# Strassen pairs for the mixer's in and out projections in a hybrid decoder layer

## Chip, cores and metric

One NeuronCore of a Trainium2 chip runs the whole kernel. The metric is the device time of one execution in microseconds (us). The engines are named as in the profile: PE is TensorE (PEld its weight loads), DVE is VectorE, ACT is ScalarE, POOL is GpSimd and SP is SyncE, which issues most DMAs.

## What is computed

One layer of a hybrid decoder on 256 tokens, with model width 2048 and FFN width 5632:

```python
x = x + 0.5 * swiglu(rmsnorm(x, ffn1_norm), w_gate1, w_up1, w_down1)   # FFN 1
h = rmsnorm(x, mix_norm)
a_q, a_k, a_v, m_q, m_k, m_v, m_o, m_i, m_f = split(h @ w_in)          # in projection
y_a = diff_attention(a_q, a_k, a_v, lam)    # 4 heads, causal, two softmaxes a head, RMSNorm
y_b = mlstm(silu(conv(m_q, m_k)), m_v, gates(m_i, m_f)) * sigmoid(m_o) # 4 heads, conv over 4 tokens
x = x + concat(y_a, y_b) @ w_out                                       # out projection
x = x + 0.5 * swiglu(rmsnorm(x, ffn2_norm), w_gate2, w_up2, w_down2)   # FFN 2
out = rmsnorm(x, final_norm)
```

All arrays are float32. The part between the two FFNs is called the mixer here.

## The kernel before

**Products.** The 256 tokens are two blocks of 128. An activation is kept transposed, as sixteen K tiles of 128 features (44 for the FFN's inner width). A product takes a 128x128 piece of the activation as the stationary operand and 512 columns of a weight, and adds into a PSUM bank of 512 columns (tag `acc`, six banks). Every operand is split in two, a rounded high part and the remainder, and each product is three matmuls: high by high, high by low, low by high (`mm3`, lines 141 to 143). Two tiles of K are a unit (UK = 2). For each unit of 512 columns, SP loads 128x1024 values of weight, ACT casts them to the high part `wh` (L113), and DVE subtracts to get the low part `wl` (L114). A transposed activation gets its parts from L108/L109 (with a gain) or L113/L114.

**Strassen pairs.** The FFNs use `Paired` (L322). It takes two weight chunks `wa` and `wb` of 512 columns and, over the first 2·ns of the K tiles, multiplies the 2x2 blocks (two token blocks by two adjacent K tiles, and two K tiles by two weight chunks) with seven block products where eight are needed plainly. The rest of K is plain. For this DVE forms sums of weight tiles, `sums` (L350) and a second sum in place (L352), which are then split like weights; a POOL DMA that adds while it copies (L361) makes a third one. The activations are needed as eight combinations, `xs`, formed by `sum_pair` (ACT `xg`/`hg`, three `xsum` operations at L273 to L275, then casts and subtractions into `xs`) in place of the two plain tiles `xt`. `combine` (L364) has six operations on the four banks of products.

**The chain.** `Chain.run` (L444) works off one pair: the first four products of each of the ns K pairs (`first`, on banks p5, p7, p1, p6), with the previous pair's `third` (the plain rest of its `wb`) between them; then `combine`; then `second` (the remaining three products, and the plain rest of `wa`), whose result goes to a function `half`; and the pair's own `third` goes into the chain for the next run. `pending` is a list of transposes that `flush` runs at one later point, so that TensorE doesn't wait for what they transpose.

**The mixer.** None of its projections is a pair. `linear` and `units` (L174, L213) work off one chunk of 512 columns after the other, each sixteen K tiles by two token blocks, 96 instructions of 128x512: three narrower chunks `wqk` (m_q, m_k and the gates), ten chunks `win`, four chunks `wout`. The mLSTM and the attention stand between the chunks: the convolution on DVE (L626 to L629), the gates between units of the first two `win` chunks, the scores (L774 to L788) and numerators (L799 to L810) of all four heads after them, the attention's scores and softmax (L833 to L867) after the q and k chunks, its weighting (L885 to L899) after the v chunks, and the gated output (L903 to L917). `rsq` (L224) raises to the power -1/2 on POOL.

**Order.** Each engine runs its instructions in program order, and a tile scheduler sets this order from the order of the code and from priorities: what stands under `tc.high_priority(offset=AHEAD)` (loads, splits) is moved ahead by up to 400 places. Pools set how far ahead work can go: 4 tiles `raw` of 1 MB, 5 `rawp` of 512 KB (which `sums` also takes), 4 split weight tiles in `wsp`, 2 banks `ps_tr` for transposes, 6 `ps_acc`.

## Time and profile before

| | us |
|---|---|
| median of three runs | 1829.08 |
| the three runs | 1822.75, 1829.08, 1830.97 |
| the profiled execution | 1824.08 |
| its span, first to last instruction | 1822.4 |
| mean granted TensorE clock in it | 0.998 |

The span is what the trace covers; 1.7 us of the profiled execution lie around it. In the trace FFN 1 runs until about 700 us, the in projection and the attention until about 1025, the out projection until about 1130, and FFN 2 from there on. Line numbers of rows are those of the kernel before. The profile's duration of an instruction reaches from its start to its end, and the next one on the engine often starts before that end; where the pace of an engine is wanted, starts are compared.

### The profile page before, as it was taken

Reading aid. Unit: us, or ns where it says so; the run is one execution under the profiler, and the core shown is the slowest. Engines: PE = TensorE matmul, PEld = TensorE weight load, DVE = VectorE, ACT = ScalarE, POOL = GpSimd, SP = SyncE. Lnnn points to the kernel's source line nnn. Section 1 sums busy time; section 2 is a strip of 40 time slices with the busy share of each in tenths; the row PEclk is TensorE's granted clock in tenths of the full one; section 3 lists DMA queues with packets and bytes.
Section 4 is the critical chain, followed back from the end, with each engine's and each line's share of the span. In section 5 each row is a group of like instructions: output and inputs, shape, how many; then the busy total and the mean of one; then the engine's idle time right before and its main releaser. Section 6 shows DMA issues by size and latency. Waiting matters only on the chain.

```text
span 1822.4 us, 22684 instructions
## 1 busy us (share of the span) xinstructions
PE 1794.6 (98%) x8090; PEld 1468.2 (81%) x8090; DVE 1488.8 (82%) x1775; ACT 1121.7 (62%) x1443; POOL 156.3 (9%) x199
## 2 busy tenths in 40 slices
PE   8999999999999999999999999999999999999998
PEld 6788788878887888978888888788787888887886
DVE  6889889988998887674465578899889988998886
ACT  6666666666666666554455456666666666666664
POOL 0001100111002100000000000101110021002100
PEclk9999999999999999999999999999999999999999
DMA  8667877797688874553544565677877798678864
GB/s 333 215 204 235 222 234 232 246 250 220 210 252 247 259 237 146 200 185 121 185 159 164 185 213 179 199 228 241 234 230 225 256 247 243 208 230 256 253 190 155
DMA packets 114449, 397.72 MB, mean 218 GB/s; under 512 B 12960, under 2 KB 12960, under 8 KB 107424
## 3 DMA queue, kind: packets, MB, share of 16 engines
q1 hardware_dynamic: 88560, 349.28, 55.5%
q0 software_dynamic: 24480, 44.58, 14.2%
q10 hardware_dynamic: 1296, 2.42, 0.4%
q8 instruction: 63, 1.03, 0.2%
q14 instruction: 50, 0.41, 0.1%
HBM read 349.56 MB, written 2.10 MB: 193 GB/s over the span
## 4 chain that ended last, share of the span: by engine, by line
PE 76%; DMA 9%; DVE 8%; issue 4%; ACT 2%; SPq 1%; POOL 0%; POOLq 0%; DVEq 0%; ACTq 0%
PE acc L142 24%; PE acc L143 24%; PE acc L141 24%; DMA raw<-in_wu_dram 6%; DVE wl L114 5%; ACT wh L113 2%; DVE sums L350 2%; DMA raw<-raw 1%; PE tr L296 1%; SPq L166 1%; DMA xres<-in_x_dram 1%; DVE raw L352 1%; DMA xraw<-in_xt_dram 1%; DMA raw<-in_wd_dram 0%; PE num L808 0%
## 5 line engine op out<-in xcount | busy, mean ns | idle before, releaser
L113 ACT CAST wh<-raw 128x1024 fp32r<-128x1024 f32 (+3 forms) x503 | 464.3, 931 | 377.2 <-PE acc L143 360.9
L114 DVE TENSOR_TENSOR wl<-raw,wh 128x1024 fp32r<-128x1024 f32 (+3 forms) x503 | 535.1, 1074 | 194.7 <-ACT wh L113 191.1
L142 PE MATMUL acc<-wl,xt 128*128 128x512 f32 (+3 forms) x1632 | 630.4, 386 | 4.2 <-DVE wl L114 4.0
L141 PE MATMUL acc<-wh,xt 128*128 128x512 f32 (+3 forms) x1632 | 630.7, 387 | 2.6 <-ACT xt L108 1.5
L143 PE MATMUL acc<-wh,xt 128*128 128x512 f32 (+3 forms) x1632 | 628.8, 386 | 1.2 <-DVE xt L109 1.2
L114 DVE TENSOR_TENSOR wl<-rawp,wh 128x1024 fp32r<-128x1024 f32 x284 | 346.7, 1222 | 43.8 <-ACT wh L113 37.1
L113 ACT CAST wh<-rawp 128x1024 fp32r<-128x1024 f32 x284 | 298.8, 1053 | 117.1 <-PE acc L143 96.4
L141 PE MATMUL acc<-wh,xs 128*128 128x512 f32 x902 | 355.7, 397 | 8.4 <-ACT wh L113 4.0
L142 PEld LDWEIGHTS acc<-wl,xt 128*128 128x128 f32 x1632 | 306.5, 188 | 67.9 <-DVE wl L114 8.8
L141 PEld LDWEIGHTS acc<-wh,xt 128*128 128x128 f32 x1632 | 306.0, 188 | 65.5 <-ACT wh L113 2.8
L143 PEld LDWEIGHTS acc<-wh,xt 128*128 128x128 f32 x1632 | 306.3, 188 | 62.1 <-DVE xt L109 2.5
L142 PE MATMUL acc<-wl,xs 128*128 128x512 f32 x902 | 352.7, 391 | 1.3 <-DVE wl L114 1.1
L143 PE MATMUL acc<-wh,xs 128*128 128x512 f32 x902 | 350.9, 390 | 0.1
L113 ACT CAST wh<-sums 128x1024 fp32r<-128x1024 f32 x122 | 128.4, 1053 | 144.4 <-PE acc L143 139.2
L141 PEld LDWEIGHTS acc<-wh,xs 128*128 128x128 f32 x902 | 169.1, 188 | 57.2 <-ACT u L371 9.3
L142 PEld LDWEIGHTS acc<-wl,xs 128*128 128x128 f32 x902 | 169.4, 188 | 38.9 <-DVE wl L114 6.4
L143 PEld LDWEIGHTS acc<-wh,xs 128*128 128x128 f32 x902 | 169.3, 188 | 36.0 <-DVE xs L109 1.0
L361 POOL DMA_DIRECT2D raw<-raw x122 | 104.0, 853 | 1030.9 <-DVE wl L114 973.7
L350 DVE TENSOR_TENSOR sums<-raw 128x1024 f32<-128x1024 f32 x122 | 149.2, 1223 | 39.4 <-DMA raw<-in_wu_dram 29.2
L114 DVE TENSOR_TENSOR wl<-sums,wh 128x1024 fp32r<-128x1024 f32 x122 | 149.0, 1222 | 14.7 <-ACT wh L113 14.7
L352 DVE TENSOR_TENSOR raw<-sums,raw 128x512 f32<-128x512 f32 x122 | 83.8, 687 | 0.5
L282 POOL DMA_DIRECT2D xres<-part x48 | 43.6, 1060 | 238.2 <-ACT part L281 238.2
(194 smaller groups left out, 756.0 us busy)
## 6 DMA issues: line engine op xcount, KB each, us to landing
rawp<-in_wd_dram SPq DMA_DIRECT2D x96, 512.0 KB, 5.7
rawp<-in_wu_dram SPq DMA_DIRECT2D x94, 512.0 KB, 7.6
raw<-in_wg_dram SPq DMA_DIRECT2D x89, 512.0 KB, 6.7
rawp<-in_wg_dram SPq DMA_DIRECT2D x86, 512.0 KB, 5.7
raw<-in_wu_dram SPq DMA_DIRECT2D x82, 512.0 KB, 7.5
raw<-in_wd_dram SPq DMA_DIRECT2D x80, 512.0 KB, 6.3
raw<-in_win_dram SPq DMA_DIRECT2D x40, 1024.0 KB, 4.8
raw<-raw POOLq DMA_DIRECT2D x122, 256.0 KB, 6.3
```

The lines of the kernel that those rows point to most:

```text
L113: nc.scalar.copy(hi, src)
L114: nc.vector.tensor_tensor(out=lo, in0=src, in1=hi.bitcast(F32), op=ALU.subtract)
L141: nc.tensor.matmul(acc, lh, rh, start=first, stop=False, skip_group_check=on)
L142: nc.tensor.matmul(acc, lh, rl, start=False, stop=False, skip_group_check=on)
L143: nc.tensor.matmul(acc, ll, rh, start=False, stop=last, skip_group_check=on)
L166: nc.sync.dma_start(dst, w[k // LK][:, k % LK:k % LK + 2, :])
L282: nc.gpsimd.dma_start(xres[:, hb, c * CW:(c + 1) * CW], t, accum_op=ALU.add)
L296: nc.tensor.transpose(tr[:, i, hb * P:(hb + 1) * P], hs[hb][:, k * P:(k + 1) * P], ident)
L350: nc.vector.tensor_tensor(out=sums, in0=raw[:, 0:4:3, :], in1=raw[:, 2:3, :].to_broadcast([P, 2, CW]), op=ALU.add)
L352: nc.vector.tensor_tensor(out=raw[:, 2, :], in0=sums[:, 0, :], in1=raw[:, 3, :], op=ALU.add)
L361: nc.gpsimd.dma_start(raw[:, 2, :], raw[:, 1, :], accum_op=ALU.add)
```

## The change

The in and out projections become Strassen pairs in the chain, as in the FFNs, with four K pairs each (NP_MIX = NP_OUT = 4: K tiles 0 to 7 by seven products, 8 to 15 plain). The ten `win` chunks are five pairs, run in the order (2,3) for a_q, (0,1) for m_v, (4,5) for a_k, (6,7) for a_v, (8,9) for the gates m_o; the four `wout` chunks are two. The first two `wqk` chunks stay plain and the third is the stream that the first pair takes between its products. The narrow chunks keep their number of instructions.

The steps of mLSTM and attention become entries of two lists: `side` (convolution of a head, gate steps) is taken up between units of `first` and `second`, and `mid` (scores, numerators, attention and weighting of one head) after each unit of `second`. Their operations on ACT and DVE go through `vec` and `act`, which raise their priority above that of the splits. Transposes in `pending` are run one per unit. The convolution's first tap moves from DVE to ACT, and the gates' small products from `ps_acc` to `ps_tr`.

`finish1` asks `chunk_to_xt` for the combinations `xs` in place of plain `xt` for half of the K tiles of the in projection, and `y_transposes` does it for the attention's four heads. In the `wout` pairs (`by_dma`) the second weight sum isn't made by DVE: ACT copies the first sum into place (L377 after) and a POOL DMA adds the other part onto it (L378 after), and the split of it is issued after the chain's unit.

```diff
+NP_MIX = 4
+NP_OUT = 4
...
-    def flush():
-
-        for f in pending:
+    def flush(n=None):
+
+        now = pending[:n]
+        del pending[:n]
+        for f in now:
             f()
...
-                sum_pair(xp, j, gained(tr, gbase + 2 * j))
+                sum_pair(xp, j, gained(tr, prm[:, gbase + 2 * j:gbase + 2 * j + 2]))
...
-            nc.scalar.activation(g[:, i * S:(i + 1) * S], src[:, i, :], AF.Copy,
-                                 scale=prm[:, gcol + i:gcol + i + 1])
+            act.activation(g[:, i * S:(i + 1) * S], src[:, i, :], AF.Copy, scale=gain[:, i:i + 1])
...
+    class Early:
+
+
+        def __init__(self, engine):
+            self.engine = engine
+
+        def __getattr__(self, op):
+            def run(*args, **kwargs):
+                with soon():
+                    return getattr(self.engine, op)(*args, **kwargs)
+
+            return run
+
+    vec, act = Early(nc.vector), Early(nc.scalar)
+    side, mid = [], []
+
+    def aside(work):
+
+        if work:
+            work.pop(0)()
+
...
                     nc.vector.tensor_tensor(out=sums, in0=raw[:, 0:4:3, :],
                                             in1=raw[:, 2:3, :].to_broadcast([P, 2, CW]), op=ALU.add)
-                    nc.vector.tensor_tensor(out=raw[:, 2, :], in0=sums[:, 0, :], in1=raw[:, 3, :], op=ALU.add)
-                    e = pair_tiles(wsp, "w", [P, 2, CW])
+                    if self.by_dma:
+                        nc.scalar.copy(raw[:, 2, :], sums[:, 0, :])
+                        nc.gpsimd.dma_start(raw[:, 2, :], raw[:, 3, :], accum_op=ALU.add)
+                    else:
+                        nc.vector.tensor_tensor(out=raw[:, 2, :], in0=sums[:, 0, :], in1=raw[:, 3, :], op=ALU.add)
+                        e = pair_tiles(wsp, "w", [P, 2, CW])
                     split(sums, *f)
-                    split(raw[:, 0:3:2, :], *e)
+                    if not self.by_dma:
+                        split(raw[:, 0:3:2, :], *e)
                 self.prod(self.p5, j, S1, f, 0, at, end)
                 self.prod(self.p7, j, S3, f, 1, at, end)
+                if self.by_dma:
+                    yield
+                    with tc.high_priority(offset=AHEAD):
+                        e = pair_tiles(wsp, "w", [P, 2, CW])
+                        split(raw[:, 0:3:2, :], *e)
                 self.prod(self.p1, j, A1, e, 0, at, end)
                 self.prod(self.p6, j, S2, e, 1, at, end)
                 with tc.high_priority(offset=AHEAD):
                     nc.gpsimd.dma_start(raw[:, 2, :], raw[:, 1, :], accum_op=ALU.add)
-                yield
+                if not self.by_dma:
+                    yield
 
         def combine(self):
...
+                aside(side)
                 if i < self.ns:
                     bare(i)
                     if i % 2 or i == self.ns - 1:
                         upper(i - i % 2)
                 if i < len(self.rest):
                     self.plain(self.wa, self.rest[i], (n11, n21))()
-                if i == 0:
+                if i % 2 == 0:
                     flush()
+                aside(mid)
             return [n11, n21]
 
         def third(self, last_units=1):
...
+        def run(self, p, half, end, last_units=1, lead=()):
 
             done = 0
+            for f in lead:
+                next(self.stream)
+                done += 1
+                f()
             for i, _ in enumerate(p.first()):
                 while done < (i + 1) * self.steps // p.ns:
                     next(self.stream)
                     done += 1
+                flush(1)
+                aside(side)
             p.combine()
             self.end()
             half(p.second())
...
-        pending.append(functools.partial(chunk_to_xt, c, G_MIX, xp2, 0))
+        pending.append(functools.partial(chunk_to_xt, c, G_MIX, xp2, NP))
...
+    def conv(acc, src, h, i):
+        w = lambda j: prm[:, G_CW + j * 8 + i:G_CW + j * 8 + i + 1]
+        a = acc[:, h, :]
+        act.activation(a, src[:, h, :], AF.Identity, scale=w(3), bias=prm[:, G_CB + i:G_CB + i + 1])
+        for d in (1, 2, 3):
+            vec.scalar_tensor_tensor(a[:, d:], src[:, h, :S - d], w(3 - d), a[:, d:], op0=ALU.mult, op1=ALU.add)
+        act.activation(a, a, AF.Silu)
...
+    accs = []
+    chain.put(units(accs, xp2, wqk[2], KD, fine=True), KD // UK, functools.partial(finish_qk, 2, accs))
...
-        mb = ps_acc.tile([P, CW], F32, tag="acc", name="mb")
+        mb = ps_tr.tile([P, CW], F32, tag="tr", name="mb")
...
+    def both(c):
+        return Paired(xp2, win[c], win[c + 1], KD, NP_MIX)
+
+    mq, mk = (mixt([P, NH, S], name="cv") for _ in range(2))
+    for i in range(2 * NH):
+        side.append(functools.partial(conv, (mq, mk)[i // NH], mT[i // NH], i % NH, i))
+    for i, f in ((1, gates_sum), (3, gates_scan), (5, gates_max)):
+        side.insert(i, f)
+    qT, kT = [], []
+    chain.run(both(2), to_T(qT), to_T(qT))
+
...
+    by_head(scores)
+    chain.run(both(0), functools.partial(take_mv, 0), functools.partial(take_mv, 1))
+    by_head(numerators)
+    chain.run(both(4), to_T(kT), to_T(kT))
...
+        pending_T.append(functools.partial(weights_T, h, w))
...
+            pending.extend([f for f in pending_T] + [lambda: mid.extend(weigh)])
...
+        if kt // 2 < NP_OUT:
+            sum_pair(yT, kt // 2, gained(tr, g))
+            return
...
+        later.append(functools.partial(y_transposes, [y[:, hb, :] for hb in range(NT)], 2 * h, gatt))
...
+    by_head(attend)
+    chain.run(both(6), take_av, take_av)
+    chain.run(both(8), functools.partial(gate_out, 0), functools.partial(gate_out, 1))
+    pending[:0] = later
...
-    for c in range(4):
-        accs = []
-        chain.put(units(accs, yT, wout[c], KD, fine=c == 3), KD // UK, functools.partial(finish_out, c, accs))
-        if c < 3:
-            chain.finish()
+    for c in (0, 2):
+        chain.run(Paired(yT, wout[c], wout[c + 1], KD, NP_OUT, by_dma=True), functools.partial(finish_out, c),
+                  functools.partial(finish_out, c + 1),
+                  lead=() if c else [functools.partial(flush, 1)] * 2)
```

Three places in the order of instructions, each word for word.

On TensorE where the out projection begins, before: `acc_8264` and `acc_8263` are the last chunk of the in projection, `tr_8318` and `tr_8328` the first transposes of attention outputs (`ya`).

```order
L142 MATMUL acc_8264<-wl_8302,xt_6003 128x512
L143 MATMUL acc_8264<-wh_8301,xt_6003 128x512
L877 MATMUL tr_8318<-ident,ya_8212 128x128 x4
L877 MATMUL tr_8328<-ident,ya_8228 128x128 x4
L141 MATMUL acc_8263<-wh_8357,xt_6013 128x512
L142 MATMUL acc_8263<-wl_8358,xt_6013 128x512
```

The same place after: `acc_8355` is the last bank of the gate pair's `third`, `acc_8859` and `acc_8858` are the first products of the first `wout` pair, on the combinations `xs_8810` and `xs_8811` made of the first head's transposes (`tr_8802`, thirteen rows further up).

```order
L145 MATMUL acc_8355<-wh_8822,xt_6238 128x512
L945 MATMUL tr_8838<-ident,ya_8671 128x128 x4
L945 MATMUL tr_8877<-ident,ya_8715 128x128 x4
L945 MATMUL tr_8923<-ident,ya_8771 128x128 x4
L945 MATMUL tr_8987<-ident,yb_8777 128x128 x4
L143 MATMUL acc_8859<-wh_8863,xs_8810 128x512
L144 MATMUL acc_8859<-wl_8864,xs_8810 128x512
L143 MATMUL acc_8858<-wh_8863,xs_8810 128x512
L144 MATMUL acc_8858<-wl_8864,xs_8810 128x512
L145 MATMUL acc_8859<-wh_8863,xs_8811 128x512
```

Three heads' transposes and the first of the mLSTM's now stand in a row right ahead of the first products that use such combinations; before, plain products of the in projection's last chunk follow two of them.

On DVE at that place, before: splits of the last chunk's weights (`wl`), and plain low parts `xt` of the attention outputs.

```order
L114 TENSOR_TENSOR wl_8410<-raw_8407,wh_8409 128x1024
L882 SCALAR_TENSOR_TENSOR xt_8317<-tr_8318,gatt,xt_8317 128x256
L882 SCALAR_TENSOR_TENSOR xt_8327<-tr_8328,gatt,xt_8327 128x256
L882 SCALAR_TENSOR_TENSOR xt_8317<-tr_8318,gatt,xt_8317 128x256
L882 SCALAR_TENSOR_TENSOR xt_8327<-tr_8328,gatt,xt_8327 128x256
L114 TENSOR_TENSOR wl_8426<-raw_8407,wh_8425 128x1024
L882 SCALAR_TENSOR_TENSOR xt_8337<-tr_8338,gatt,xt_8337 128x256
L882 SCALAR_TENSOR_TENSOR xt_8347<-tr_8348,gatt,xt_8347 128x256
```

After: the splits of the first `wout` pair's weights, and the combinations (`xs`, `xsum`) of four heads.

```order
L116 TENSOR_TENSOR wl_8910<-sums_8911,wh_8909 128x1024
L116 TENSOR_TENSOR xs_8811<-xg_8807,xs_8810 128x512
L116 TENSOR_TENSOR wl_8942<-raw_8906,wh_8941 128x1024
L275 TENSOR_TENSOR xsum_8814<-xg_8807 128x256
L276 TENSOR_TENSOR xsum_8814<-xsum_8814,xg_8807 128x128
L277 TENSOR_TENSOR xsum_8814<-xg_8807,xsum_8814 128x128
L275 TENSOR_TENSOR xsum_8850<-xg_8843 128x256
L276 TENSOR_TENSOR xsum_8850<-xsum_8850,xg_8843 128x128
L116 TENSOR_TENSOR xs_8847<-xg_8843,xs_8846 128x512
L277 TENSOR_TENSOR xsum_8850<-xg_8843,xsum_8850 128x128
L275 TENSOR_TENSOR xsum_8889<-xg_8882 128x256
L116 TENSOR_TENSOR xs_8811<-xsum_8814,xs_8810 128x512
```

Where two low parts were formed for a pair of K tiles, five instructions stand now, between splits that the first products wait for.

On POOL, before, from the mLSTM's norm to FFN 2's first pair: `rmh` and four `ra` alone.

```order
L224 TENSOR_TENSOR rmh_7149<-rsqv_7147,mhalf 128x8
L224 TENSOR_TENSOR ra_8210<-rsqv_8208,mhalf 128x2
L224 TENSOR_TENSOR ra_8226<-rsqv_8224,mhalf 128x2
L224 TENSOR_TENSOR ra_8242<-rsqv_8240,mhalf 128x2
L224 TENSOR_TENSOR ra_8258<-rsqv_8256,mhalf 128x2
L361 DMA raw_9148<-raw_9148 128x512
```

After, the same stretch up to the second `wout` pair: L378 is the added DMA of `by_dma`, L395 the DMA that makes the third sum, L227 the power for a head's norm.

```order
L378 DMA raw_8860<-raw_8860 128x512
L227 TENSOR_TENSOR ra_8613<-rsqv_8611,mhalf 128x2
L378 DMA raw_8906<-raw_8906 128x512
L227 TENSOR_TENSOR ra_8669<-rsqv_8667,mhalf 128x2
L227 TENSOR_TENSOR ra_8713<-rsqv_8711,mhalf 128x2
L378 DMA raw_8952<-raw_8952 128x512
L378 DMA raw_9008<-raw_9008 128x512
L395 DMA raw_8860<-raw_8860 128x512
L227 TENSOR_TENSOR ra_8769<-rsqv_8767,mhalf 128x2
L395 DMA raw_8906<-raw_8906 128x512
L395 DMA raw_8952<-raw_8952 128x512
L395 DMA raw_9008<-raw_9008 128x512
```

Four DMAs of `by_dma` stand ahead of the first L395 of that pair, and `ra` of the attention heads stands between them.

## Rows read from the trace of the kernel before

**Rows 1.** The page: busy time of each engine, its share of the span and its instructions; then the chain of work that ended last, by engine.

```profile
PE 1794.6 (98%) x8090; PEld 1468.2 (81%) x8090; DVE 1488.8 (82%) x1775; ACT 1121.7 (62%) x1443; POOL 156.3 (9%) x199
...
PE 76%; DMA 9%; DVE 8%; issue 4%; ACT 2%; SPq 1%; POOL 0%; POOLq 0%; DVEq 0%; ACTq 0%
```

**Rows 2.** What TensorE waited for over the whole run: line, what it waited for: us in total, times, longest.

```profile
PE acc L142 <- DVE wl L114: 5.1, 12, 0.8
PE acc L141 <- ACT wh L113: 4.9, 9, 0.7
PE acc L141 <- ACT xs L108: 2.0, 2, 1.5
```

**Rows 3.** The same view, from 705 to 1120 us, which is the mixer without its last part: all that it lists.

```profile
PE tr L242 <- DVE xt L109: 0.2, 1, 0.2
```

**Rows 4.** Busy time of each engine in stretches: the first FFN's middle, the mixer up to its last part, the last part of the output projection with the hand-over to the second FFN, the second FFN's middle. Columns: stretch and its length, then PE, PEld, DVE, ACT and POOL busy us (instructions), the granted TensorE clock (1.00 is 2.4 GHz, 0.50 is 1.2 GHz), DMA share, GB/s.

```profile
250.00:700.00 450.00, 447.12 (x1985) 364.90 (x1984) 404.33 (x446) 288.82 (x344) 48.02 (x60) 1.00 0.79 236
705.00:1120.00 415.00, 414.72 (x2003) 349.08 (x2002) 250.50 (x385) 221.62 (x346) 8.90 (x12) 1.00 0.50 172
1120.00:1165.00 45.00, 43.03 (x189) 33.95 (x188) 37.76 (x44) 27.75 (x36) 4.65 (x5) 1.00 0.63 192
1165.00:1700.00 535.00, 531.09 (x2358) 434.07 (x2357) 487.37 (x537) 346.78 (x411) 61.82 (x73) 1.00 0.78 234
```

**Rows 5.** TensorE's timeline in an input-projection chunk: start, duration, line, tile. A matmul's records overlap; the starts of those left out lie between the rows shown at the same pace, and the last row is the 44th after the first.

```profile
803.74 0.39 PE L141 MATMUL acc<-wh,xt 128*128 128x512 f32 x1
803.97 0.40 PE L142 MATMUL acc<-wl,xt 128*128 128x512 f32 x1
804.20 0.39 PE L143 MATMUL acc<-wh,xt 128*128 128x512 f32 x1
...
813.50 0.39 PE L142 MATMUL acc<-wl,xt 128*128 128x512 f32 x1
813.73 0.39 PE L143 MATMUL acc<-wh,xt 128*128 128x512 f32 x1
```

**Rows 6.** The two FFN stretches again, with the instructions on tiles named acc alone (columns as above; the count behind PE is that of the matmuls).

```profile
250.00:700.00 450.00, 442.09 (x1921) 357.69 (x1920) 46.68 (x71) 33.23 (x56) 1.00 0.79 236
1165.00:1700.00 535.00, 525.43 (x2286) 425.95 (x2285) 50.25 (x77) 40.70 (x70) 1.00 0.78 234
```

**Rows 7.** The same for tiles named tr, the 128x128 transposes.

```profile
250.00:700.00 450.00, 8.28 (x64) 7.46 (x64) 5.91 (x9) 8.97 (x16) 1.00 0.79 236
1165.00:1700.00 535.00, 9.31 (x72) 8.41 (x72) 5.91 (x9) 10.11 (x18) 1.00 0.78 234
```

**Rows 8.** Three stretches around the mLSTM's scores and numerators, which stand between two projection chunks (columns as in the stretches above, with the granted clock behind POOL).

```profile
814.00:822.00 8.00, 8.00 (x39) 5.34 (x39) 2.90 (x4) 4.44 (x13) 0.00 (x0) 0.99 0.52 196
822.00:825.20 3.20, 3.20 (x10) 2.55 (x10) 1.05 (x3) 0.61 (x3) 0.00 (x0) 0.50 0.00 0
825.20:829.00 3.80, 3.80 (x20) 3.34 (x18) 2.77 (x12) 0.00 (x0) 0.00 (x0) 1.00 0.00 0
```

**Rows 9.** VectorE's timeline inside a Strassen pair of the second FFN, instructions back to back.

```profile
1183.85 1.22 DVE L114 TENSOR_TENSOR wl<-rawp,wh 128x1024 fp32r<-128x1024 f32 x1
1184.99 1.22 DVE L350 TENSOR_TENSOR sums<-raw 128x1024 f32<-128x1024 f32 x1
1186.12 0.29 DVE L275 TENSOR_TENSOR xsum<-hg,xsum 128x128 f32<-128x128 f32 x1
1186.33 0.69 DVE L352 TENSOR_TENSOR raw<-sums,raw 128x512 f32<-128x512 f32 x1
1186.93 1.22 DVE L114 TENSOR_TENSOR wl<-sums,wh 128x1024 fp32r<-128x1024 f32 x1
1188.06 1.22 DVE L114 TENSOR_TENSOR wl<-raw,wh 128x1024 fp32r<-128x1024 f32 x1
```

**Rows 10.** VectorE's groups of equal instructions: line, operation, out<-in, shapes xcount | busy us, mean ns of one | idle before.

```profile
L372 DVE TENSOR_TENSOR acc<-acc,u 128x512 f32<-128x512 f32 x37 | 25.6, 693 | 0.5 <-ACT u L371 0.5
L114 DVE TENSOR_TENSOR xs<-xsum,xs 128x512 fp32r<-128x512 f32 x28 | 19.0, 686 | 0.0
L109 DVE SCALAR_TENSOR_TENSOR xt<-tr,prm,xt 128x256 fp32r<-128x256 f32 x24 | 10.6, 479 | 0.6 <-ACT xt L108 0.5
L273 DVE TENSOR_TENSOR xsum<-hg 128x256 f32<-128x256 f32 x20 | 8.4, 420 | 0.0
L626 DVE TENSOR_SCALAR cv<-mT,prm 128x256 f32<-128x256 f32 x8 | 3.2, 407 | 0.0
L898 DVE TENSOR_SCALAR ya<-av,ra 128x256 f32<-128x256 f32 x8 | 3.5, 480 | 3.4 <-POOL ra L224 3.4
```

**Rows 11.** The same view of ScalarE.

```profile
L113 ACT CAST wh<-rawp 128x1024 fp32r<-128x1024 f32 x284 | 298.8, 1053 | 117.1 <-PE acc L143 96.4 <-ACT wh L113 10.5 <-issue 2.3
L113 ACT CAST wh<-raw 128x512 fp32r<-128x512 f32 x132 | 77.9, 620 | 87.6 <-PE acc L143 86.1 <-DMA raw<-in_wg_dram 1.5
L371 ACT COPY u<-acc 128x512 f32<-128x512 f32 x37 | 21.4, 579 | 0.6 <-DVE acc L370 0.4
L257 ACT ACTIVATE xg<-tr,prm 128x256 f32<-128x256 f32 x8 | 3.3, 467 | 0.0
```

**Rows 12.** GpSimd's instructions on tiles named raw (the DMAs that add one quarter of a weight tile onto another, all from L361): ns of one min/median/max, first and last start; then the time from issue to landing.

```profile
L361 POOL DMA_DIRECT2D raw<-raw x122: 841/854/1038, 44.4 to 1780.5; - x122
DMA to landing us min/median/max: 3.3/6.3/9.9
```

More of the change, by code (lines that the diff above doesn't have):

```diff
@@ L168, in load_unit @@
     def load_unit(w, k):
-        raw = wrp.tile([P, UK, CW], F32, tag="rawp", name=nm("rawp"))
+        raw = wrp.tile([P, UK, w.shape[3]], F32, tag="rawp", name=nm("rawp"))
         with tc.high_priority(offset=AHEAD):
@@ L538, in sum_xt @@
         raw, j, hi, lo = gs.pop(0)
-        sums(gained(raw, G_FFN1 + j * UK), hi, lo)
+        sums(gained(raw, prm[:, G_FFN1 + j * UK:G_FFN1 + j * UK + UK]), hi, lo)
     parts1 = small.tile([P, NT, 4], F32, tag="parts", name="parts1")
@@ L750, in gates_max, with take_mv, scores @@
             mcol = ct([P, 8], "mcol")
-            nc.vector.tensor_tensor(out=mcol, in0=mm[:, 0:8], in1=bcol[:, 0:8], op=ALU.add)
+            vec.tensor_tensor(out=mcol, in0=mm[:, 0:8], in1=bcol[:, 0:8], op=ALU.add)
             enm = ct([P, 8], "enm")
-            nc.scalar.activation(enm, mcol, AF.Exp, scale=-1.0)
+            act.activation(enm, mcol, AF.Exp, scale=-1.0)
         late.update(enm=enm)
-    mq = conv_silu(mT[0], 0)
-    mk = conv_silu(mT[1], 4)
-    between = {(0, 4): gates_sum, (0, 6): gates_scan, (1, 4): gates_max}
     mv = {}
-    for j in range(2):
-        accs = linear(xp2, win[j], KD, ahead=lambda u: between.get((j, u), lambda: None)())
+    def take_mv(j, accs):
         for hb in range(NT):
-            t = mixt([P, 2, VD + 1], name="mv")
+            t = work.tile([P, 2, VD + 1], F32, tag="w", name=nm("mv"))
             mv[j, hb] = t
             nc.gpsimd.memset(t[:, :, VD:VD + 1], 1.0)
-            nc.scalar.activation(t[:, :, 0:VD], accs[hb].rearrange("p (a b) -> p a b", a=2), AF.Copy,
+            act.activation(t[:, :, 0:VD], accs[hb].rearrange("p (a b) -> p a b", a=2), AF.Copy,
                                  scale=rstd2()[:, hb:hb + 1])
-    gcol, gx, nsel, mrow, enm = (late[n] for n in ("gcol", "gx", "nsel", "mrow", "enm"))
+    def both(c):
[7 more added lines that the diff above has]
+    chain.run(both(2), to_T(qT), to_T(qT))
     sws = []
-    for h in range(NH):
+    def scores(h):
+        gcol, gx, nsel, mrow = (late[n] for n in ("gcol", "gx", "nsel", "mrow"))
         rr = ps_acc.tile([P, CW], F32, tag="acc", name=nm("rr"))
@@ L822, in tile_trunk_layer, with attend @@
     fm = ct([P, 8], "fm")
[L823 to L830 removed]
+    vec.tensor_tensor(out=fm, in0=rmh, in1=dd, op=ALU.mult)
     sca = DK ** -0.5
[L832 to L833 removed]
+    wts, weigh = {}, []
+    def attend(h):
         q, k, o = qT[h // 2], kT[h // 2], 2 * (h % 2)
```

206 lines of the change are left out of this document (95 added, 111 removed).

## Prediction

> **What bounds the kernel now.** First the page's totals and its chain of waits: TensorE is busy for 98% of the span, and 76% of the chain that ended last is PE [rows 1]. VectorE, 82% busy, is next. So the first question is how many matmul slots the change removes, the second whether the other engines still keep ahead. The list of what TensorE waited for has no entry of weight [rows 2], and in the mixer nearly none at all: 0.2 us in 415 [rows 3]. The stretches show why. In the mixer DVE is busy for 250.50 of 415 us (60%) and ACT for 221.62 (53%), while the FFNs, which run on Strassen pairs already, have DVE at 404.33 of 450 and 487.37 of 535 (90 and 91%) [rows 4]. The FFN stretches are thus the best picture of what the mixer becomes.
>
> **What a matmul slot is worth.** Records overlap, so the pace is read from starts: 803.74 to 813.73 is 9.99 us for 44 steps, 0.227 us each [rows 5]. A pair of chunks needs 16 K tiles x 2 chunks x 2 token blocks x 3 = 192 instructions plainly. As a pair with four K pairs it needs 4 x 7 x 3 = 84, and 8 x 2 x 2 x 3 = 96 for the plain rest, 180 together. Seven pairs save 84 instructions: 84 x 0.227 = **-19.1 us**. All of this lies on the path, since PE is what never waits there.
> The row's pace is that of a stream in which every matmul has a weight load of its own. The Trainium skill ("TensorE: Matmul & The Clock Gate", section "Back-to-back issue gap") gives about 131 ns as the sustained spacing of matmuls with 512 columns, and about 216 ns as an isolated one. By 131 ns the 84 would bring 11.0 us and the sum below would be 8.1 us higher; the trace speaks against it, and for the page's other figure, with 44 equal steps of 227 ns.
>
> **The clock.** Between two chunks the scores and numerators of all heads stand in a row, and in 822.0 to 825.2 the granted clock is 0.50, which is 1.2 GHz, after a stretch at 0.99 that was filled with narrow matmuls; behind it the clock is 1.00 again [rows 8]. After the change each head's scores and numerators follow a unit of full-width products. I expect the drop not to come: half of 3.2 us, **-1.6 us** (bounds 0 and -1.6).
>
> **Stalls where DVE is tight.** In the first FFN stretch 450 us hold 1921 wide matmuls, 1921 x 0.227 = 436.1, and 8.28 us of transposes; 5.6 us are left over. In the second: 535 - 2286 x 0.227 - 9.31 = 6.8 [rows 6, 7]. Both are 1.25% of the stretch. The mixer pays nearly nothing of that now. Is its DVE load going to be like theirs? Back to back, a DVE instruction starts 0.08 us before the last one's end: 1.14 us for 128x1024, 0.60 for 512 columns, 0.21 for the small `xsum` [rows 9]. A pair in the in projection has per K pair `sums`, the second sum, two splits of 1024, later one more split of 1024 and one of 512: 4 x 1.14 + 2 x 0.60 = 5.76, four times 23.0; eight plain units 9.1; `combine` 4 x 0.61 = 2.4 [rows 9, 10]. That is 34.6 us beside 180 x 0.227 = 40.9 of PE, where the two plain chunks had 16 x 1.14 = 18.2: +16.3 a pair. A `wout` pair leaves out the second sum, 4 x 0.60, and has +13.9. Five and two pairs: +109. Eight activation pairs change from two `xt` (0.40 each) to two `xs` and three `xsum` (2 x 0.60 + 0.34 + 2 x 0.21 = 1.96): +9.3. The convolution's first tap leaves DVE, 8 x 0.33 = -2.6 [rows 10]. So about +116 on 250.5, 366 us in a stretch that shrinks to some 404: 91%, the FFNs' load. ACT gains the casts and copies for the same tiles (1.05, 0.62, 0.58 and 0.47 us [rows 11]), about +77 on 221.6, 74%: not the bound on average. I therefore give the mixer the FFNs' share: 1.25% of 400 = **+5 us** (bounds 0 and 12: none, as now, or 16 steps of the heads that each cost one of the longest single waits seen, 0.8 us [rows 2]).
>
> **The start of the out projection.** Here the work isn't like the FFNs'. The first `wout` pair needs sums of attention outputs that come from transposes just ahead, and the order has four groups of transposes in a row, through two banks, then the first products. I count from the order, from the first TensorE row that uses the unit before the last of the gate pair's rest up to the end of the first part of that `wout` pair: 96 wide matmuls and 24 transposes (8.28 / 64 = 0.13 us each [rows 7]), 21.8 + 3.1 = 24.9 us. DVE has in that time 12 splits and 2 `sums` of 1024 (16.0), eight `xs` parts (4.8), four groups of `xsum` (3.0), ten operations of 256 columns (4.0) and two tiny ones (0.2): 28.0 us. DVE is 3.1 us behind if it starts level. Before, TensorE had plain products there, and what waited was DVE, for `ra` on POOL, 3.4 us in four waits [rows 10]. POOL now issues four adding DMAs (0.85 us each [rows 12]) among these `ra`, and each delay of one passes on to `ya`, the transposes and the sums. I take **+3 us** (bounds 0, if DVE enters with tiles ready, and 8: the 3.1, the four `ra` waits of 3.4 and one or two POOL issues of 0.85 in front).
>
> **The two ends.** At FFN 1's end the transposes of the first two chunks of x feed four `sum_pair`s and not plain tiles, inside the last pair of FFN 1: 4 x 1.16 = 4.6 us more on a DVE that is 90% busy, most of it ahead of need: **+1** (0 to 3). At the hand-over to FFN 2 the stretch of 45 us has 43.03 of PE [rows 4], so 2 us are lost already; the last `wout` chunk's rest still ends inside FFN 2's first pair, now beside sums and a `combine` on DVE: **+1** (-2, if nothing is lost there any more, to 3). Loads cost nothing: the weight bytes are the same, and the DMA share in the mixer is 0.50 where the FFNs run at 0.79 with loads of the same size [rows 4]. The 36 further POOL DMAs at 0.85 us are 31 us on an engine with 9% load [rows 1, 12].
>
> **Sum against the profiled execution:** -19.1 - 1.6 + 5 + 3 + 1 + 1 = -10.7, so 1824.08 becomes 1813.4. The three runs before lie on average 3.5 us above it (1827.6; their median 5.0 above). I add 3.5: **1817 us**, case A.
>
> **Rivals.**
> B, the stalls don't come: the steps of the heads fill what DVE leaves, and DVE enters the out projection with work in hand. For it: the three longest entries of TensorE's waits sum to 12 us in the whole run [rows 2], fewer than 1.25% of it. Against: every stretch on pairs shows its 1.25%. -19.1 - 1.6 = -20.7: 1803.4, with 3.5 about 1807.
> C, bursts: sixteen steps (scores, numerators, attention, weighting of four heads) stand on TensorE in line between wide products, and each has an answer from ACT or DVE that the next one needs. Their raised priority puts them ahead of splits, and a split that is late stops TensorE. Now such steps wait in the plain mixer for little [rows 3], since DVE has 40% free; at 91% it hasn't. At 0.5 us a step, between 0.2 [rows 3] and 0.8 [rows 2], this is 8 us more: 1821.4, with 3.5 about 1825, no difference that counts.
> D, slower, by `by_dma`: the second sum of a `wout` unit takes an ACT copy (0.58), a POOL issue (0.85), the landing (6.3 in the median, 3.3 to 9.9), a cast (1.05) and a split (1.22), 10.0 us in a row [rows 9 to 12], while TensorE has 24 x 0.227 = 5.45 us of work per unit. If POOL's queue or the five `rawp` tiles keep these from running ahead, each unit costs 4.5 us and eight cost 36: 1850, about 1853. It decides from five such units on (5 x 4.5 = 22 above A's 1817 is 0.5% over the old time). Against: the order puts four of these DMAs ahead of the first other one in the first `wout` pair, so they run ahead of the products that need them.
> The Trainium skill ("SBUF — State Buffer", section "SBUF: two separate sides") warns that a DMA issued from GpSimd can starve while VectorE holds the port that they share, and that would lengthen D's chain with VectorE at 91%. In the FFNs, at 90%, the trace has the issue at 841 to 1038 ns throughout, which leaves D's terms as they are.
> That the change doesn't do what it says is ruled out by the instructions: 84 fewer wide matmuls stand in its order.
>
> **Chances.** A 0.45, B 0.17, C 0.28, D 0.10. About 0.5% (9.1 us) is what a measurement of this kernel can tell from no change: below 1820 is faster, above 1838 slower. A lies near that bound, and 0.08 of its 0.45 falls inside; C all but does. Faster 0.37 + 0.17 = 0.54, same 0.08 + 0.28 = 0.36, slower 0.10. The range goes from B less the 4 us that runs scatter, 1803, to C with the start of the out projection at its upper bound, 1825 + 5 + 2 = 1832.
>
> **What would show it.** In the stretches after: the mixer's PE near its length, DVE near 90% there, and no 0.50 clock at the scores. TensorE's waits in the in projection some 5 us, on `wl` and `wh`, spread out; if they gather at the heads' tiles, C. Around the first `wout` product a wait for `xs` of some 3 us; if TensorE waits there for `wl` whose tile waits on a `raw<-raw` landing, several times 4 us, D. The forecast is wrong if the pace of wide matmuls isn't 0.227 us in pairs, or if the FFNs lose time through a pool or a queue that the new mixer leaves full.

## The result

| | before | after |
|---|---|---|
| median of 17 runs each | 1825.35 us | 1833.88 us |
| lowest to highest | 1821.06 to 1830.97 | 1826.93 to 1838.96 |
| span of the profiled execution | 1822.4 | 1833.7 |

The ratio is 1.0042, with a 95% interval of 1.003 to 1.0054. The kernel is 0.4% slower; 1817 was forecast, with a range up to 1832, and the median lies 1.9 us above that range.

The page of after, busy time and the chain that ended last, answers to [rows 1]:

```profile
PE 1784.4 (97%) x8006; PEld 1452.3 (79%) x8006; DVE 1600.1 (87%) x1923; ACT 1186.8 (65%) x1553; POOL 186.5 (10%) x235
...
PE 66%; DMA 12%; DVE 11%; issue 6%; ACT 3%; SPq 1%; POOL 0%; POOLq 0%; DVEq 0%; ACTq 0%
```

TensorE works 10 us less than before and the span is 11 us longer. So its idle time grew by 21 us: the matmuls are gone, and what was saved was lost again in waits. What it waited for, whole run, beside [rows 2]:

```profile
PE acc L144 <- DVE wl L116: 12.8, 22, 1.9
PE acc L143 <- ACT wh L115: 8.4, 11, 1.1
PE acc L143 <- ACT xs L115: 2.8, 1, 2.8
PE tr L245 <- DVE xres L289: 2.2, 2, 1.9
```

Where, in stretches of the two kernels (columns as in [rows 4]). Before:

```profile
700.00:725.00 25.00, 24.94 (x126) 21.50 (x125) 17.80 (x29) 16.61 (x31) 1.03 (x3) 1.00 0.25 83
725.00:1000.00 275.00, 274.78 (x1356) 232.09 (x1355) 155.02 (x264) 141.65 (x231) 4.43 (x5) 0.99 0.47 167
1000.00:1025.00 25.00, 25.00 (x116) 20.80 (x115) 14.90 (x19) 13.89 (x18) 0.00 (x0) 1.00 0.55 205
1025.00:1050.00 25.00, 25.00 (x116) 20.79 (x115) 14.68 (x17) 12.61 (x19) 0.00 (x0) 1.00 0.48 171
1050.00:1125.00 75.00, 75.00 (x345) 62.28 (x344) 56.99 (x69) 44.13 (x61) 3.45 (x4) 1.00 0.63 196
```

After:

```profile
700.00:725.00 25.00, 22.98 (x101) 18.59 (x100) 22.50 (x40) 19.70 (x37) 0.00 (x0) 0.93 0.12 39
725.00:1000.00 275.00, 272.57 (x1338) 227.77 (x1338) 233.56 (x353) 184.53 (x296) 23.34 (x32) 1.00 0.67 202
1000.00:1025.00 25.00, 20.26 (x89) 16.08 (x88) 20.65 (x37) 18.68 (x32) 4.93 (x6) 0.86 0.53 146
1025.00:1050.00 25.00, 23.65 (x110) 19.10 (x109) 22.17 (x33) 18.13 (x28) 1.70 (x2) 1.00 0.52 159
1050.00:1125.00 75.00, 67.45 (x297) 52.60 (x297) 64.58 (x78) 47.38 (x70) 9.37 (x11) 1.00 0.75 218
```

Reading them: from 725 to 1000, the in projection with the steps, TensorE lacks 2.4 us of 275, and the clock is 1.00 where it was 0.99. VectorE went from 155 to 234 us there, 85% of the stretch, and that costs next to nothing. These are its two largest waits there; only the first, for VectorE's `den`, ends with an operation of the heads' steps:

```profile
PE acc L143 <- DVE den L330: 1.1, 1, 1.1
PE acc L144 <- DVE wl L116: 0.9, 2, 0.8
```

The loss is in the other four rows. At FFN 1's end (700 to 725) 2.0 us are idle; at 1000 to 1125, the out projection with its start, 4.7 + 1.4 + 7.5 = 13.6 us, where before had none. In marks that both traces have: between FFN 1's last transposes of its inner activation `sg` (681.3 before, 681.9 after) and FFN 2's first (1174.8, 1183.7) the mixer went from 493.5 to 501.8 us. From there FFN 2 took 602.9 and 604.1 up to its last transposes.

At FFN 1's end the order of the transposes of x differs. Before, the sixteen came in two lots of eight, with thirteen wide products between them:

```profile
703.78 1.04 PE L242 MATMUL tr<-ident,xres 128*128 128x128 f32 x8
707.86 1.06 PE L242 MATMUL tr<-ident,xres 128*128 128x128 f32 x8
```

After, they stand in a row from 699.61 on, and the second eight wait for the banks of the first:

```profile
701.65 0.66 PE L245 MATMUL tr<-ident,xres 128*128 128x128 f32 x4 [1.00 <-ACT xg L330]
702.99 0.66 PE L245 MATMUL tr<-ident,xres 128*128 128x128 f32 x4 [0.68 <-ACT xg L330]
```

The idle time isn't all of it. The granted clock in two short stretches of after, at FFN 1's end and at the longest wait (columns as above, the clock is the third number from the end):

```profile
704.00:708.00 4.00, 4.00 (x11) 3.13 (x12) 4.00 (x8) 3.38 (x8) 0.00 (x0) 0.57 0.02 4
1016.00:1022.00 6.00, 4.30 (x10) 3.22 (x11) 5.65 (x17) 3.79 (x7) 0.89 (x1) 0.50 0.43 105
```

The timeline of TensorE at the second of these, where the first product of the out projection follows the row of transposes that the order shows (start, duration, what; in brackets the idle time before it):

```profile
1010.62 1.03 PE L945 MATMUL tr<-ident,ya 128*128 128x128 f32 x8
1012.82 0.65 PE L945 MATMUL tr<-ident,ya 128*128 128x128 f32 x4 [1.17 <-ACT xg L330]
1014.21 0.66 PE L945 MATMUL tr<-ident,yb 128*128 128x128 f32 x4 [0.73 <-ACT xg L330]
1017.70 0.79 PE L143 MATMUL acc<-wh,xs 128*128 128x512 f32 x1 [2.84 <-ACT xs L115]
1018.29 0.63 PE L144 MATMUL acc<-wl,xs 128*128 128x512 f32 x1
1018.72 0.63 PE L143 MATMUL acc<-wh,xs 128*128 128x512 f32 x1
```

Two waits for ScalarE's gained copies stand between transposes, since both banks are taken. Then 2.84 us pass until the first `xs` is there. The products behind it start 0.43 us apart, where 0.227 is the pace [rows 5]. It is the lower of the two clock levels, and it costs another 0.2 us for each of about ten products. In the trace this level is granted from 1015.2 to 1022.0, so it begins inside the wait. Counting as in [rows 6, 7], wide matmuls and then transposes of this part of after:

```profile
1000.00:1125.00 125.00, 105.10 (x431) 80.23 (x430) 9.29 (x14) 4.75 (x8) 0.97 0.66 192
```

```profile
1000.00:1125.00 125.00, 8.45 (x56) 6.64 (x56) 3.75 (x8) 10.63 (x25) 0.97 0.66 192
```

431 x 0.227 = 97.8, 8.45 of transposes and 1.46 of the attention's narrow products: of 125 us 17 are left. Before, the same count, 533 matmuls and 5.18 us of transposes, comes to 126 us (those at the edges counted whole) and leaves nothing, so this part lost about 18 us. The forecast had given it some 4. The pace itself holds in pairs: from the first to the second of these rows of after, in the in projection, are 101 steps in 22.97 us, 0.227 us each.

```profile
859.12 0.39 PE L145 MATMUL acc<-wh,xs 128*128 128x512 f32 x1
882.09 0.39 PE L144 MATMUL acc<-wl,xt 128*128 128x512 f32 x1
```

### The profile page after: what moved, and what is told of

Read it like the earlier page. It is cut to its first block, busy times and chain, and to the rows that moved or that the text cites. A ratio compares the mean times of both kernels' runs of the same rounds, so it can differ in the third digit from the quotient of the medians.

```text
span 1833.7 us, 23080 instructions
## 1 busy us (share of the span) xinstructions
PE 1784.4 (97%) x8006; PEld 1452.3 (79%) x8006; DVE 1600.1 (87%) x1923; ACT 1186.8 (65%) x1553; POOL 186.5 (10%) x235
## 4 chain that ended last, share of the span: by engine, by line
PE 66%; DMA 12%; DVE 11%; issue 6%; ACT 3%; SPq 1%; POOL 0%; POOLq 0%; DVEq 0%; ACTq 0%
PE acc L144 22%; PE acc L145 21%; PE acc L143 21%; DMA raw<-in_wu_dram 7%; DVE wl L116 6%; DVE sums L374 2%; ACT wh L115 2%; DMA raw<-raw 2%; DMA raw<-in_wd_dram 1%; SPq L169 1%; PE tr L298 1%; DMA raw<-in_win_dram 1%; DMA raw<-in_wout_dram 1%; DVE raw L380 0%; DMA raw<-in_wg_dram 0%
## 5 line engine op out<-in xcount | busy, mean ns | idle before, releaser
L144 PE MATMUL acc<-wl,xt 128*128 128x512 f32 (+2 forms) x1360 | 528.7, 389 | 5.7 <-DVE wl L116 5.4
L143 PE MATMUL acc<-wh,xt 128*128 128x512 f32 (+2 forms) x1360 | 526.5, 388 | 3.8 <-ACT wh L115 2.2
L145 PE MATMUL acc<-wh,xt 128*128 128x512 f32 (+2 forms) x1360 | 526.5, 388 | 0.5 <-DVE xt L111 0.5
L143 PE MATMUL acc<-wh,xs 128*128 128x512 f32 (+2 forms) x1146 | 452.1, 397 | 14.9 <-ACT wh L115 6.2
L144 PE MATMUL acc<-wl,xs 128*128 128x512 f32 (+2 forms) x1146 | 446.2, 389 | 7.4 <-DVE wl L116 7.4
L116 DVE TENSOR_TENSOR wl<-rawp,wh 128x1024 fp32r<-128x1024 f32 (+1 forms) x340 | 410.5, 1209 | 49.0 <-ACT wh L115 40.9
L115 ACT CAST wh<-rawp 128x1024 fp32r<-128x1024 f32 (+1 forms) x340 | 354.4, 1043 | 147.2 <-PE acc L145 118.7
L145 PE MATMUL acc<-wh,xs 128*128 128x512 f32 (+2 forms) x1146 | 444.2, 389 | 0.1
L144 PEld LDWEIGHTS acc<-wl,xt 128*128 128x128 f32 x1360 | 255.8, 188 | 63.7 <-DVE wl L116 12.3
L143 PEld LDWEIGHTS acc<-wh,xt 128*128 128x128 f32 x1360 | 255.2, 188 | 58.8 <-ACT wh L115 4.3
L145 PEld LDWEIGHTS acc<-wh,xt 128*128 128x128 f32 x1360 | 255.7, 188 | 52.5 <-DVE xt L111 1.4
L143 PEld LDWEIGHTS acc<-wh,xs 128*128 128x128 f32 x1146 | 215.4, 188 | 74.2 <-ACT u L406 10.4
L144 PEld LDWEIGHTS acc<-wl,xs 128*128 128x128 f32 x1146 | 216.0, 188 | 53.6 <-DVE wl L116 14.6
L395 POOL DMA_DIRECT2D raw<-raw x150 | 128.6, 857 | 1206.9 <-DVE wl L116 994.7
L145 PEld LDWEIGHTS acc<-wh,xs 128*128 128x128 f32 x1146 | 215.3, 188 | 44.6 <-DVE xs L116 1.2
```

The lines of the kernel that those rows point to most:

```text
L115: nc.scalar.copy(hi, src)
L116: nc.vector.tensor_tensor(out=lo, in0=src, in1=hi.bitcast(F32), op=ALU.subtract)
L143: nc.tensor.matmul(acc, lh, rh, start=first, stop=False, skip_group_check=on)
L144: nc.tensor.matmul(acc, lh, rl, start=False, stop=False, skip_group_check=on)
L145: nc.tensor.matmul(acc, ll, rh, start=False, stop=last, skip_group_check=on)
L395: nc.gpsimd.dma_start(raw[:, 2, :], raw[:, 1, :], accum_op=ALU.add)
```

## Experiments

Two theories. **Handover**: the loss sits at single places where TensorE needs something that was made just ahead (sums of fresh transposes, sums by way of a DMA, a late load), and each can be mended apart. **Load**: VectorE at 90% with the steps' bursts costs everywhere about the same, and a place that is mended moves its loss elsewhere. All ratios are to the kernel before, each to runs of it made beside the experiment, and a gain over after or over another experiment is the difference of the two ratios, taken of 1825 us.

**1. In projection alone.** The out projection goes back to plain chunks.

```diff
-NP_OUT = 4
+NP_OUT = 0
...
-    for c in (0, 2):
-        chain.run(Paired(yT, wout[c], wout[c + 1], KD, NP_OUT, by_dma=True), ...
+    for _ in range(4):
+        next(chain.stream)
+        flush(1)
+    chain.finish()
+    for c in range(4): ...   # as in the kernel before
```

> The in projection stays on pairs; the out projection is four plain chunks again, with plain transposed tiles. Handover theory (the loss sits where sums are made of fresh transposes and in the two out-projection pairs): TensorE gets 24 x 0.227 = 5.4 us of matmuls back, and the 7.6 us of stalls at 1000 to 1025, 1.9 at 1025 to 1050 and about 11 at 1050 to 1125 go: about 14 us less than the changed kernel, 5 less than the one before. Load theory (VectorE at 90% costs everywhere alike, 27 us over some 400): a quarter of the stalls, 7 us, goes for 5.4 us of matmuls: within 2 us of the changed kernel, 7 over the one before.

Measured: 1817.87, ratio 0.9949 (0.9932 to 0.9965): 17 us better than after. Its stretches:

```profile
1000.00:1025.00 25.00, 25.00 (x124) 20.78 (x123) 17.69 (x28) 15.97 (x26) 0.70 (x1) 1.00 0.24 85
1025.00:1050.00 25.00, 24.88 (x120) 20.56 (x119) 14.95 (x19) 14.19 (x23) 0.00 (x0) 1.00 0.51 177
1050.00:1125.00 75.00, 75.00 (x345) 62.19 (x344) 59.67 (x75) 45.95 (x66) 3.44 (x4) 1.00 0.60 191
```

TensorE has 0.1 us of idle time left from 1000 to 1125, and from 725 to 1000 it is busy for 272.33 of 275 us, as in after. The out projection's two pairs save 5.4 us of matmuls and cost some 22. The edit also spreads the attention's transposes, one lot behind each of four units, so the 22 include the row of transposes at the start, which experiment 5 takes up by itself.

**2. The second weight sum on VectorE** (`by_dma` off).

```diff
-Paired(yT, wout[c], wout[c + 1], KD, NP_OUT, by_dma=True)
+Paired(yT, wout[c], wout[c + 1], KD, NP_OUT)
```

> The second weight sum of the out-projection pairs is made by VectorE as in all other pairs, not by a ScalarE copy and an adding DMA. If the chain copy, DMA, cast, split is what stops TensorE in the out projection: ScalarE's 5.8 us of waits on that DMA go, and 5 us or more of the 11 us of stalls at 1050 to 1125. If it is the handover or the load: no gain, up to 3 us more, since VectorE has 8 x 0.60 = 4.8 us more to do there.

Measured: 1829.87, ratio 1.0019 (1.0004 to 1.0033), 4 us better than after; the two intervals overlap slightly. What ScalarE waited for from 1023 to 1140, after:

```profile
ACT wh L115 <- DMA raw<-raw: 5.8, 2, 3.8
ACT wh L115 <- DMA rawp<-in_wout_dram: 3.7, 1, 3.7
```

and in this experiment only the second kind:

```profile
ACT wh L115 <- DMA rawp<-in_wout_dram: 6.5, 2, 4.2
```

The adding DMA was a wait and is gone, but loads for the plain rest come late in its place. TensorE's idle time from 1050 to 1125 fell from 7.5 to 5.2 us, not by the 5 us expected. So the chain of rival D is in the trace, though small: two waits of ScalarE and not eight. This profile also has no low clock at 700 to 725 where after had it, in a part that the edit doesn't touch; up to 1.6 us of the 4 may be that.

The longest wait of TensorE here, and the stretch behind it (columns as in [rows 4]):

```profile
1109.03 0.88 PE L245 MATMUL tr<-ident,xres 128*128 128x128 f32 x6 [2.93 <-DVE xres L289]
1109.00:1115.00 6.00, 5.97 (x33) 5.12 (x34) 5.22 (x10) 5.93 (x12) 0.00 (x0) 1.00 0.25 44
```

It is as long as the 2.84 us of after, and the clock behind it is 1.00.

**3. Steps at normal priority.**

```diff
-    vec, act = Early(nc.vector), Early(nc.scalar)
+    vec, act = nc.vector, nc.scalar
```

> The steps' operations on ScalarE and VectorE keep their normal priority, so that they no longer go ahead of the splits. If the steps' bursts in front of splits cost TensorE its time: 5 us less or better, with fewer waits on wl and wh in the in projection. Handover theory: the in projection's waits are small (about 9 us in 275), so 0 to 3 us less at best, and later answers to TensorE's narrow products may cost 5 to 20 us more.

Measured: 1837.01, ratio 1.0057 (1.0038 to 1.0077). Not better, 3 us worse by the medians, with overlapping intervals. The raised priority isn't what costs the time: without it TensorE's idle time from 725 to 1000 is 4.9 us in place of 2.4. Rival C's price of 8 us isn't there either, since in the in projection of after the one wait of weight that ends with an operation of the heads' steps is 1.1 us long.

**4. FFN 1's end in two lots.**

```diff
-                flush(1)
+                if p.ns > 1:
+                    flush(1)
...
-                if i % 2 == 0:
+                if self.ns == 1:
+                    flush(1)
+                elif i % 2 == 0:
                     flush()
```

> At FFN 1's end the sixteen transposes come in two lots of eight with a unit of wide products between them, all else as changed. Handover theory: the 4.4 us of stalls at 700 to 725 (2.5 of waits for ScalarE's gained copies and 1.6 of products at half clock behind them) fall to about 1: 3 us less than the changed kernel. Load theory: the same work in another place, no change within 1 us.

Measured: 1829.77, ratio 1.0017 (1.0005 to 1.0029): 4.5 us better than after. The stretch at FFN 1's end:

```profile
700.00:725.00 25.00, 25.00 (x127) 21.76 (x126) 22.43 (x42) 22.14 (x41) 0.68 (x1) 1.00 0.23 74
```

No idle time, full clock, with as much VectorE work there as in after. It was the order, not the load: the edit restores the two lots that the kernel before had.

**5. Attention's transposes early.** They join the list when a head is weighted, and run between units of the gate pair.

```diff
-        later.append(functools.partial(y_transposes, ...
+        pending.append(functools.partial(y_transposes, ...
-    pending[:0] = later
```

> The transposes of the attention outputs go into the list as soon as a head is weighted, so that they run between units of the gate pair and not in a row ahead of the first out-projection products; all else as changed. Handover theory: of the 7.6 us of stalls at 1000 to 1025 (2 us between the transposes, 3.0 for the first sum, 2.1 of products at half clock behind that) at most 2 stay: 4 to 6 us less than the changed kernel, and the granted clock of 0.50 at 1016 to 1022 doesn't come. If the wait is the load on VectorE in that stretch and not the order, the same amount of work stops TensorE elsewhere: within 2 us of the changed kernel.

Measured: 1828.92, ratio 1.0016 (1.0007 to 1.0025): 4.8 us better than after. The start of the out projection, in which after had a clock of 0.50 at 1016 to 1022:

```profile
1000.00:1016.00 16.00, 14.24 (x62) 11.34 (x61) 14.59 (x29) 13.53 (x23) 4.10 (x5) 0.89 0.48 115
1016.00:1022.00 6.00, 6.00 (x30) 4.86 (x29) 6.00 (x10) 5.52 (x9) 0.90 (x1) 1.00 0.84 234
```

Idle 1.8 us here and none in the second stretch. The low clock isn't gone, as had been expected: it now comes from 1011.7 to 1015.1, 3.4 us where after had 6.8, and the first products on `xs`, from 1012.12 on, run 0.43 us apart in it. Some waits remain ahead of the second stretch, for `ya` and for the first splits. As in experiment 2, this profile has the full clock at FFN 1's end, so up to 1.6 us of the 4.8 may be that.

**6. Edits 2, 4 and 5 together.**

> Out-projection pairs kept, with the three edits together: transposes at FFN 1's end in two lots, attention transposes early, second weight sum on VectorE. If the three losses are separate places: 4 + 4 + 5 = 13 us less than the changed kernel, 4 less than the one before, still 5 to 6 us of stalls in the out projection's body. If what is mended moves on to the next wait: 8 us less or fewer.

Measured: 1820.68, ratio 0.9976 (0.9963 to 0.9988): 12 us better than after. The three add up within what the intervals can tell (4.2 + 4.5 + 4.8 = 13.5, with the low clock at FFN 1's end perhaps counted more than once), as separate places do. From 1050 to 1125 TensorE is still idle for 4.7 us. Its timeline at the longest wait:

```profile
1097.16 0.39 PE L145 MATMUL acc<-wh,xs 128*128 128x512 f32 x1
1100.47 1.54 PE L245 MATMUL tr<-ident,xres 128*128 128x128 f32 x6 [2.92 <-DVE xres L289]
1101.67 0.78 PE L143 MATMUL acc<-wh,xs 128*128 128x512 f32 x1
1102.24 0.63 PE L144 MATMUL acc<-wl,xs 128*128 128x512 f32 x1
1102.67 0.63 PE L145 MATMUL acc<-wh,xs 128*128 128x512 f32 x1
```

and VectorE's just before:

```profile
1096.72 1.22 DVE L374 TENSOR_TENSOR sums<-raw 128x1024 f32<-128x1024 f32 x1
1097.99 1.22 DVE L116 TENSOR_TENSOR wl<-raw,wh 128x1024 fp32r<-128x1024 f32 x1
1099.13 0.68 DVE L380 TENSOR_TENSOR raw<-sums,raw 128x512 f32<-128x512 f32 x1
1099.73 1.88 DVE L289 SCALAR_TENSOR_TENSOR xres<-acc,xres 128x512 f32<-128x512 f32 x3
```

The products of that bank end at about 1097.5. VectorE has a sum, a split and another sum queued ahead of the residual (L289) and reaches it at 1099.73. The transposes wait 2.92 us, and the products behind start 0.43 apart again. In experiment 2 the same wait, 2.93 us, had no such stretch behind it.

**7. In projection alone, with edit 4.**

> Plain out projection, in projection on pairs, and FFN 1's transposes in two lots. Handover theory: 60 instructions fewer are 13.6 us, less 1.6 us of clock at the scores, and some 3 us of new waits in the in projection: 12 us less than the kernel before, 4 less than with the plain out projection alone. Load theory: no more than with the plain out projection alone, 9 us less than before.

Measured: 1815.53, ratio 0.9935 (0.9922 to 0.9947), 12 us better than before, as the handover theory has it; the interval is 9.7 to 14.2 us, just clear of the load theory's 9. Against experiment 1 it is 2.6 us with overlapping intervals, so 4 can't be told from nothing in the times. In the profile the loss at FFN 1's end is gone: TensorE is busy for 25.00 us from 700 to 725 at full clock, where experiment 1 has 23.34 at 0.93.

**8. Edit 6, and the residual of the out projection at the steps' priority** (a scale of 1.0 marks this projection).

```diff
-            nc.vector.scalar_tensor_tensor(xs, accs[hb], scale, xs, op0=ALU.mult, op1=ALU.add)
+            (vec if scale == 1.0 else nc.vector).scalar_tensor_tensor(xs, accs[hb], scale, xs, op0=ALU.mult, op1=ALU.add)
```

> The three mended places kept, and the addition of the out projection to x on VectorE gets the steps' priority. Queue theory: the transposes of x wait (1.1 and 3.1 us, and half clock behind the second) because this addition stands behind splits and sums on VectorE; then these waits nearly go, 3 to 4 us less than the three mended places. If it is VectorE's load: the splits that now come later stop TensorE instead, no change within 1.5 us.

Measured: 1819.88, ratio 0.997 (0.9954 to 0.9985); 1.1 us better than edit 6, less than the interval can tell. TensorE's two largest waits from 1000 to 1140, and its stretch from 1050 on:

```profile
PE acc L145 <- DVE xt L111: 2.0, 2, 1.3
PE tr L948 <- DVE ya L330: 1.3, 1, 1.3
1050.00:1125.00 75.00, 73.03 (x328) 57.97 (x327) 73.30 (x93) 55.06 (x82) 6.34 (x8) 1.00 0.68 204
```

The waits for `xres` are gone as the queue theory expected. Others (`xt`, 2.0 us) have come, but TensorE's idle time from 1000 to 1125 fell from 9.5 us in experiment 6 to 4.8, and no low clock is left there. The traces thus speak for the queue theory. The times don't decide: the intervals allow the 3 to 4 us that it expected as well as no change.

**9. Edit 8, and the plain rest's loads on ScalarE's queue.**

```diff
-            load_pair(raw, w, k)
+            load_pair(raw, w, k, nc.scalar if any(w is o for o in outs) else None)   # outs: the four wout chunks
```

> As e8, and the loads of the out-projection pairs' plain rest are issued on ScalarE's queue, so that on SyncE's they no longer stand behind loads that wait for a free tile. Queue theory: ScalarE's wait of 4.5 us for such a load and TensorE's of 2.5 us behind it go: 2 to 3 us less than e8. If the load is late for want of bandwidth or of a free tile of its own: no gain, and a ScalarE that holds such a load up to 3 us worse.

Measured: 1825.04, ratio 0.9997 (0.9985 to 1.0009): 5 us worse than edit 8. The gain that the queue theory of these loads expected didn't come. Since the edit also puts the issues between ScalarE's own instructions, it doesn't show that the place in SyncE's queue was harmless. TensorE now waits longer for sums and splits:

```profile
PE acc L145 <- DVE xs L116: 3.7, 1, 3.7
PE acc L144 <- DVE wl L116: 3.6, 3, 1.3
```

**10. Edit 7, and the residual at the steps' priority.**

> Plain out projection, in projection on pairs, FFN 1's transposes in two lots, and the out projection's addition to x at the steps' priority. The 4.0 us of stalls at the hand-over to FFN 2 contain at most 1 to 2 us of waits for that: 0 to 2 us less than without the priority (1815.5), 11 to 13 less than the kernel before.

Measured: 1812.64, ratio 0.9926 (0.9908 to 0.9943), the fastest of all, 13.5 us below the kernel before. Against edit 7 the 1.6 us are within the intervals. TensorE is idle for 0.1 us from 1000 to 1125. Against experiment 8, which has the out projection on pairs, it is 8.0 us better with 24 wide matmuls (5.4 us) more, and these intervals don't touch.

## Why the prediction was wrong

The saving came as forecast. The step that failed is the price of the stalls: it was taken from the average load of VectorE, +5 and +3 and +1, where single places lost about 18 us in the out projection and 4.5 at FFN 1's end. Point by point:

- **What a slot is worth** was right. 0.227 us holds in pairs too, and with the 60 instructions of the in projection (13.6 us) and the clock at the scores (1.6), 12 us were left over in experiment 7. By the 131 ns of the Trainium skill ("TensorE: Matmul & The Clock Gate", section "Back-to-back issue gap") an estimate would have been 60 x 0.131 = 7.9, with the clock 9.5 us and no room for any new wait. The trace, with 227 ns, doesn't agree with it, and the smallest gain in that experiment's interval, 0.53% or 9.7 us, is larger.
- **Stalls where DVE is tight**, +5 for the whole mixer: VectorE's load itself was forecast well (+116 us; 1488.8 became 1600.1, +111). For the in projection, with VectorE at 85%, the price was about right: 13.6 + 1.6 - 12 = 3, or 1 to 5.5 by the interval of experiment 7. The step failed in spreading one share over everything. By 1.25% the out projection's body (1050 to 1125) should have lost 0.9 us. At about the same load (64.58 of 75 us) it lost 7.5 us of idle time, a tenth of it.
- **The start of the out projection** was named with its mechanism but sized at 3 us. The single wait for `xs` that the prediction looked for came, 2.84 us long; with those around it the part showed 6.1 us of idle time at 1000 to 1050, and some 2 of low clock. I had balanced work against work over the stretch, 28.0 to 24.9 us. What counted was latency: transposes, gained copy, cast and split came one after the other, through two banks, before the first products could run. Moving the same work (experiment 5) brought 4.8 us.
- **FFN 1's end**, +1, was 4.5 by experiment 4. The same error: the sums were counted as work that lies ahead of need; what stopped TensorE were sixteen transposes in a row, through two banks. That the change would put them in a row, where the kernel before had two lots, was not in the prediction at all.
- **The clock** was taken as a gain at the scores alone. It came (0.99 to 1.00), but two new stretches at the lower level came with the new order, 3.4 us at FFN 1's end and 6.8 at the start of the out projection, which I had no term for. They don't follow every long wait: behind 1.89 and 1.92 us at 1087 and 1101 of after the clock is 1.00.
- **Hand-over to FFN 2**, +1: 45 us had 43.03 of PE before, and FFN 2 with it went from 602.9 to 604.1; 1.2 us, about the size given.
- **Rival D** has a chain that the trace shows, and its price was at most some 4 us instead of 36: the DMAs do run ahead, two of eight come late.
- **Rival C** (bursts of the steps in front of splits) is refuted for the in projection by the 2.4 us of idle time there, of which 1.1 are one wait for an operation of the heads, and experiment 3 shows that the raised priority isn't the cause.
- **The range** ended at 1832, and the last 2 us of it have no term named for them.

The sum then: -19.1 - 1.6 + 3 (in projection) + 4.5 (FFN 1's end) + about 18 (out projection from 1000 to 1125) is +5 us; with +0.6 in FFN 1, +1.2 in FFN 2 and +1.2 behind its last transposes (44.7 and 45.9) about 8. The spans differ by 11.3, the medians by 8.5; what is left of it I can't place.

What stays open: why the out projection's pairs, of the same shape as those of the in projection, still cost more than they save after all mending. In experiment 8 they keep 4.8 us of idle time from 1000 to 1125. Counted as above, 7.4 us of that stretch are left over, where experiment 10 has nothing left (517 wide matmuls and 64 transposes fill it); the rest doesn't show as idle time. Late loads stand there in the trace; giving them another queue made it worse, so their place in SyncE's queue isn't shown to be the cause. VectorE, busy for 73.30 of 75 us there in that experiment, fits too, but was not tested by itself.

## What to carry to other kernels

In this kernel an engine's average load predicted the steady part of a pipeline well and its joints not at all. At each joint (where a stage starts on operands that were made just ahead), count the latency from the last instruction that makes an operand to the first that uses it, in the order as scheduled, with the number of buffers in between. Take the change where the pipeline is steady (the in projection), leave it where its operands are just made, and spread transposes that feed a longer preparation between wide products.
